# A hybrid transformer layer: the transfers that sum weight blocks are placed behind attention weight splits, and the second feed-forward product splits two pieces ahead

## The chip, the cores and the metric

The kernel runs on one core of a Trainium2 chip. TensorE (PE) multiplies, VectorE (DVE), ScalarE (ACT) and GpSimd (POOL) work on vectors, SyncE (SP) issues most transfers; POOL and ACT can issue transfers too. The metric is the device time of one launch in microseconds (us), as a median over runs.

## The reference, cut to what matters

One layer over 512 latent tokens with a context prefix of 256 tokens, width 1024, all in float32.

```python
h_lat = modulate(x, norm1_g, sh1, sc1)            # adaLN, from c
h_ctx = modulate(ctx, norm1_g, csh1, csc1)        # from c_ctx
p_lat, p_ctx = h_lat @ w_in, h_ctx @ w_in         # z, xBC, dt, q, k, v, gates
ssd = ssd_output(ssd_bidir(...), xs, z, d_skip, g)   # bidirectional state-space mixer
att = window_ctx_attention(q, k, v, kc, vc, sink)    # window 128, all context keys
x = x + gt1 * (g_ssd * (ssd @ w_o_ssd) + g_att * (att @ w_o_att)) @ w_out
u = dwconv(modulate(x, norm2_g, sh2, sc2) @ w_up)    # 1024 -> 2 x 2816, 3 taps along tokens
x = x + gt2 * ((silu(u[:, :2816]) * u[:, 2816:]) @ w_down)
return rmsnorm(x, final_g)
```

## The kernel before

**Products.** Activations lie transposed, channels on partitions and tokens along the free axis. A float32 product is made of three float32r products: weight and activation are each split into a high part and a low part (high x high, high x low, low x high). For a weight tile this is `split`: ACT casts the raw tile to the high part (`whi`, L172), DVE subtracts it from the raw tile (`wlo`, L173). A raw tile is 128 x 1024, 512 KB, loaded by SP (`load_raw`, L166) into one of three buffers; `whi` and `wlo` have two buffers each.

**Start.** A plan written in Python (class `Plan`, with costs and due times per step) fixes the order of PE, ACT and DVE up to the first products: 16 loads of modulation weights (`wm`, L460), 8 of the input (`xsb`), 8 of a first block of gate columns (`w`), two of the context, then the first q and k weights (`wraw<-wq`, `wraw<-wk`) and the tables. Modulation rows come out of PE (L506), are copied (`tm`, L510) and turned into columns (L514); the inputs are scaled by them (`ah`, `al`), and the gate product runs on them (L556) before the RMS factor is known. POOL raises the two means to the power -0.5 (L594). ACT takes the tanh of five gate tiles (L618) in two alternating buffers `tb`, each of which SP writes to DRAM (`ts_d`, L619). Then come the normed context (`hch`, L548), the first k and q, and v.

**Attention.** A second plan orders 16 blocks of attention (scores L935, row minimum L944, exponential L951, norm of the rows L966, transposes L971, values L984) beside 30 projection products: q 2 to 7, k 1, z and the attention output. Each of these splits its weight in `high` (ACT, L1065) and `low` (DVE, L1068), and `high` issues the next weight's load. q and k rows are copied within the on-chip memory by SP (L832, L867); the plan counts 6 us for them. After it come the state-space part, with POOL's first work there at L1483 and broadcasts `fb` of decay rows from DRAM (L1552), then the output products, the up product (L216 to L219 with `mh`, `ml`) and the down product.

**Down product.** It is not done as one matrix product. The two halves of the tokens and of the 2816 and 1024 channels make blocks, and seven block products with sums of operands take the place of eight. The sums of activations are made on DVE (`f_sums`, `f_split`). The sums of weight blocks are made by transfers from DRAM to DRAM: `weight_sums` issues 32 of them on POOL's queue, 704 KB each, 16 of which copy a block into `DSUMS` and 16 of which add another block to it there (`accum_op`). It is called where the plan of the start has been written out; a scheduler orders POOL's queue, and there nothing holds the transfers back but each other:

```python
for q in range(4):
    G.dma_start(DSUMS[j][q], first[q])                              # L152
for q in range(4):
    G.dma_start(DSUMS[j][q], more[q], accum_op=ALU.add, ...)        # L154
```

`down_step(j, q)` runs block product j for one of four output tiles: two weight pieces of 6 and 5 tiles (`DPARTS`), 33 matmuls of 256 columns (`product`, L1960 to L1962). `down_last` takes the eight pieces of the last block product at once and ends with the final norm and the output. `run` walks the program of steps: before a step is written out, its pieces and one more have been loaded and split.

Of the kernel before, what the change touches and what calls it, by code (L numbers as in the profile page):

```python
# [10 lines left out]
F32R = mybir.dt.float32r  # L11
U8 = mybir.dt.uint8
AF = mybir.ActivationFunctionType
ALU = mybir.AluOpType
# [4 lines left out]
P = 128  # L19
# [4 lines left out]
EPS = 1e-6  # L24
# [6 lines left out]
V_FG = 64  # L31
# [8 lines left out]
def raw(ap):  # L40
    return ap.bitcast(F32)
# [3 lines left out]
def tile_hybrid_layer(  # L45
# [31 lines left out]
    V, S, G, T = nc.vector, nc.scalar, nc.gpsimd, nc.tensor  # L77

    cpool = ctx.enter_context(tc.tile_pool(name="cpool", bufs=1))
    wpool = ctx.enter_context(tc.tile_pool(name="wpool", bufs=2))  # L80
    hpool = ctx.enter_context(tc.tile_pool(name="hpool", bufs=1))
# [24 lines left out]
    def accb():  # L106
        return bank("acc")

    def misb():
        return bank("mis")  # L110
# [3 lines left out]
    def tmp(tag):  # L114
        return tpool.tile([P, 512], F32, tag=tag, name=tag, bufs=TMP[tag])
# [23 lines left out]
    DK = NFF // 2  # L139
    DPARTS = ((0, 6), (6, DK - 6))  # L140
    DSUMS = {i: dpool.tile([4, P, DK * P], F32, name="dsum%d" % i) for i in (1, 2, 4, 5)}
# [2 lines left out]
            for u, (k0, n) in enumerate(DPARTS):  # L144
                src["dn", (4 * j + q) * 2 + u] = t[:, k0 * P : (k0 + n) * P], n * P

    def weight_sums():
        for j, first, more in (
            (4, wdn[0], wdn[2]), (1, wdn[2], wdn[3]), (2, DSUMS[4], wdn[3]), (5, DSUMS[2], wdn[1]),
        ):  # L150
            for q in range(4):
                G.dma_start(DSUMS[j][q], first[q])  # L152
            for q in range(4):
                G.dma_start(DSUMS[j][q], more[q], accum_op=ALU.add, max_dma_last_dim=DK * P)  # L154

    M_LOADS = {}

# [12 lines left out]

    def split(r, n, hi, lo):
        S.copy(hi[:, :n], r[:, :n])  # L172
        V.tensor_tensor(lo[:, :n], r[:, :n], raw(hi[:, :n]), ALU.subtract)  # L173

    ELSEWHERE = {}

    def load(key):
        r, n = load_raw(key)
        if key[0] == "m":
            return r  # L180
        if key in ELSEWHERE:
            hi, lo = ELSEWHERE[key]()
            split(r, n, hi, lo)
            return hi, lo
        hi = wpool.tile([P, 1024], F32R, tag="whi", name="whi", bufs=2)
        lo = wpool.tile([P, 1024], F32R, tag="wlo", name="wlo", bufs=2)
        split(r, n, hi, lo)
        return hi, lo

    def run(prog, early=None):  # L190

        seq = [k for keys, _ in prog for k in keys]
        have, nload, nuse = {}, 0, 0
        for keys, fn in prog:
            nuse += len(keys)
            while nload < min(nuse + 1 + (early in keys), len(seq)):
                have[seq[nload]] = load(seq[nload])
                nload += 1
            fn(*[have.pop(k) for k in keys])
# [49 lines left out]
    def col(base, i):  # L249
        return vec[:, base + i : base + i + 1]  # L250
# [6 lines left out]
    def rms_sums(ps, part, nblk, c, first, last, late=False):  # L257
        for i in range(nblk):
            m = T.matmul(
                ps[:, i : i + 1], part[:, i * P : (i + 1) * P], rmsc[:, c : c + 1],  # L260
                start=first and i == 0, stop=last, skip_group_check=True,
            )
            if i == 0 and late:
                tc.keep_in_program_order(m)

    def rms_root(ps, nblk, eps):
        rs = cpool.tile([P, 4], F32, tag="rs", name="rs", bufs=2)
        ms = cpool.tile([P, 4], F32, tag="ms", name="ms", bufs=2)
        V.tensor_scalar_add(ms[:, :nblk], ps[:, :nblk], eps)  # L269
        G.tensor_tensor(rs[:, :nblk], ms[:, :nblk], phalf[:, :nblk], ALU.pow)  # L270
        return rs
# [110 lines left out]
    hll = hpool.tile([P, KT, L], F32R, tag="hll", name="hll")  # L382
# [17 lines left out]
    first = {}  # L400
    gates = []
    with tc.tile_pool(name="spool", bufs=1) as sp:
# [38 lines left out]
        first_, B_ = Plan(), {}  # L441
# [14 lines left out]
        mod_raw, w0_raw, wh, wl, hi_, lo_, rows, raws, ws = {}, {}, {}, {}, {}, {}, {}, {}, {}  # L456
# [101 lines left out]
        def product(j, i, t):  # L558
            h = (hi_.get(j), lo_.get(j)) if j < NU else (hlh[:, j, :], hll[:, j, :])

            n = 3 * NU if j < NU else 3 * KT
            part(pg[i], ("P", i), n, [w[j][:, i * P : (i + 1) * P] if j in w else None for w in (wh, wl)], h, t)
# [21 lines left out]
        def sums(x, q, n):  # L584
            B_["p" + x] = accb()
            rms_sums(B_["p" + x], q, n, 0, True, True)
# [51 lines left out]
        r = {}  # L638
        cq = tmp("te")[:, :LC]
        for j in range(KT):  # L640
# [46 lines left out]
            x = ("hi", "lo") if j >= NU else ("hh", "hl")  # L687
# [31 lines left out]
        for n in range(2):  # L719
            for j in range(KT):  # L720
                x = ("hi", "lo") if j >= NU else ("hh", "hl")
# [6 lines left out]
        run_plan(first_.order({"PE": 5.2, "ACT": 3.0, "DVE": 3.6, "SP": 0.7}, bus=2.76))  # L728
        first.update(w=ws[1], q=B_[0, "g"], k=B_[1, "g"])
    dump("h", raw(hlh[:, 0, :]))  # L730
    weight_sums()

# [119 lines left out]
    Q, F = {}, {}  # L854
# [187 lines left out]
    def product_atoms(g, key, accs):  # L1042

        kind, t = key
        d, R, G_ = {}, 1e6 + 100 * g, "%d" % g
# [19 lines left out]
            S.copy(d["w"][0], d["r"])  # L1065

        def low():
            V.tensor_tensor(d["w"][1], d["r"], raw(d["w"][0]), ALU.subtract)  # L1068

        def rope_part(f):  # L1070
            scale = -0.125 if kind == "k" else 1.0
# [35 lines left out]
        last, late = "G%s.7" % G_, g >= OLD  # L1107
# [524 lines left out]
    for g in range(4):  # L1632
        s = ssd_steps(g)
# [106 lines left out]
    HL = L // 2  # L1740
    HALF = [slice(0, HL), slice(HL, L)]
# [196 lines left out]
    def x_add(c, u, a, ps):  # L1938
        x = x1[c // 4][:, c % 4, HALF[u]]
        g = ng2[:, c - 4 : c - 3] if a < 0 else mod2[:, 24 + c : 25 + c]  # L1940
        V.scalar_tensor_tensor(x, ps, g, x, ALU.mult, ALU.add)

    def half_square(c, u):
        x, q = x1[c // 4][:, c % 4, HALF[u]], q3[:, HALF[u]]
        if c % 4 == 0 and (c, u) in ((0, 0), (4, 1)):
            S.activation(q, x, AF.Square)
        else:
            sq = tmp("tc")[:, :HL]
            S.activation(sq, x, AF.Square)
            V.tensor_tensor(q, q, sq, ALU.add)  # L1950
# [49 lines left out]

        return [("dn", (4 * j + q) * 2 + u) for u in range(2)], fn

    def down_last(*ws):

        ws = [ws[2 * q : 2 * q + 2] for q in range(4)]
        scaled, r = {}, {}

        def finish(u):

            z = HALF[u]  # L2010
            tail = u == 0
            r3 = rms_spread(r["s"], 2)
            if tail:
                r3s = tmp("tc")[:, :HL]
                S.copy(r3s, rms_spread(r["s"], 2)[:, :HL])
            for i, cs in enumerate(((0,), (1,), (4,), (2, 3), (5,), (6,), (7,)) if tail else ((0, 1), (2, 3), (4, 5), (6, 7))):
                for c in cs:
                    x = x1[c // 4][:, c % 4, z]
                    if tail and c in scaled:
                        G.tensor_tensor(x, scaled[c], r3s, ALU.mult)  # L2020
                    else:
                        V.scalar_tensor_tensor(x, x, col(V_FG, c), r3[:, :HL], ALU.mult, ALU.mult)
                n, c = len(cs), cs[0]
                tc.keep_in_program_order((S if c in ((1, 2, 6) if tail else (2,)) else nc.sync).dma_start(
                    out[c * P : (c + n) * P, z].rearrange("(a p) t -> p a t", a=n), x1[c // 4][:, c % 4 : c % 4 + n, z]
                ))
                yield

        pf = misb()

        def sums(u, part, first, last):
            rms_sums(pf[:, 2 * u : 2 * u + 2], part, 2, 0, first, last)

        def root():
            sums(1, q3[:, HALF[1]], True, True)
            r["s"] = rms_root(pf[:, 2:4], 2, EPS)

        def spread():
            r["f"] = finish(1)
            next(r["f"])  # L2040
            next(r["f"])

        def early():
            sums(0, q3[:, HALF[0]], False, False)
            for _ in r["f"]:
                pass

        with tc.manual_schedule(engines={mybir.EngineType.PE}):
            for q in range(4):
                ps = accb()  # L2050
                product(6, q, ws[q], ps[:, :HL], True, {1: {2: root}, 2: {2: spread}, 3: {6: early}}.get(q, {}))
                if q < 3:
                    x_add(4 + q, 0, -1, ps[:, :HL])
                    half_square(4 + q, 0)
                    if q < 2:
                        scaled[4 + q] = tmp("te")[:, :HL]
                        S.activation(scaled[4 + q], x1[1][:, q, HALF[0]], AF.Copy, scale=col(V_FG, 4 + q))
            xo, sq = x1[1][:, 3, HALF[0]], tmp("tc")[:, :HL]
            for b in range(2):
                z = slice(b * P, (b + 1) * P)  # L2060
                V.scalar_tensor_tensor(xo[:, z], ps[:, z], ng2[:, 3:4], xo[:, z], ALU.mult, ALU.add)
                S.activation(sq[:, z], xo[:, z], AF.Square)
            sums(0, sq, False, True)
            r["s"] = rms_root(pf[:, 0:2], 2, EPS)
            for _ in finish(0):
                pass

    run(
        [([], lambda: (y_split(range(8)), [square(True) for _ in range(4)], y_split(range(8, 12))))]
# [6 lines left out]
        + [([("out", o) for o in (5, 6, 7)], out_last), ([], close_c1)]  # L2076
        + weave([up_step(t) for t in range(NFF)], msteps[24:])
        + [down_step(j, q) for j in range(6) for q in range(4)]
        + [([("dn", 48 + i) for i in range(8)], down_last)],
        early=("g", 15),  # L2080
    )

# [83 lines left out]
```

## Time and profile before

| | |
|---|---|
| median of three runs | 1310.0 us (1309.07 to 1311.47) |
| profiled execution | 1307.86 us, its span 1306.1 us |
| busy: PE | 1248.7 us, 96% |
| busy: DVE, ACT, POOL | 924.3, 686.8, 169.1 us |
| POOL's transfers (q0) | 23.07 MB, 7.4% of the 16 DMA engines' span |
| SP's transfers (q1) | 181.32 MB, 44.6% |

The profile is of one execution. Busy times of PE come from modelled ends of pipelined matmuls, so a full PE is not PE at its peak. "Granted clock" is the TensorE clock as a share of full speed. A line of a view of waits reads: who waited, for whom, us in total, times, longest. The idle time of an engine that is not the bound costs nothing.

### The profile page before, as it was taken

The numbers are of one execution on the slowest core, as the hardware profiler recorded it, in microseconds if no ns is written. First come the engines' busy times: TensorE is split into PE (matmuls) and PEld (weight loads), VectorE is DVE, ScalarE is ACT, GpSimd is POOL, SyncE is SP. The second block draws the span as 40 slices with busy tenths as digits, with TensorE's granted clock in tenths as the row PEclk, the third lists the DMA queues.
The fourth block names the chain that finished last, engine by engine and source line by source line (L and its number), as shares of the span: only waits on it lengthen the run. The fifth ranks groups of instructions, "written<-read, shape, count | busy, mean of one in ns | idle before, by whom it ended". The sixth has DMA issues, their size and how long they took to land.

```text
span 1306.1 us, 18420 instructions
## 1 busy us (share of the span) xinstructions
PE 1248.7 (96%) x6790; PEld 1037.5 (79%) x6790; DVE 924.3 (71%) x1518; ACT 686.8 (53%) x1289; POOL 169.1 (13%) x177
## 2 busy tenths in 40 slices
PE   6667999999999999999999999999999999999997
PEld 4445888888888887877877778888988888889997
DVE  1244478878877358969789676777677777777785
ACT  1224477878774445648657475222543434344563
POOL 2121000000000003425244262000200000000000
PEclk7788899999999999999999999999999999999999
DMA  9999831432224723644635657777323333336553
GB/s 292 310 322 299 198 89 55 129 105 78 73 79 133 205 98 97 168 140 113 194 104 165 200 161 247 251 234 233 115 97 113 113 113 113 113 115 203 176 169 105
DMA packets 104761, 206.35 MB, mean 158 GB/s; under 512 B 8928, under 2 KB 52768, under 8 KB 104416
## 3 DMA queue, kind: packets, MB, share of 16 engines
q1 hardware_dynamic: 94736, 181.32, 44.6%
q0 software_dynamic: 8960, 23.07, 7.4%
q8 instruction: 53, 0.87, 0.3%
q10 hardware_dynamic: 976, 0.79, 0.2%
q14 instruction: 36, 0.29, 0.1%
HBM read 182.54 MB, written 40.17 MB: 171 GB/s over the span
## 4 chain that ended last, share of the span: by engine, by line
PE 89%; DMA 9%; ACT 1%; DVE 1%; issue 0%; SPq 0%; POOL 0%; DVEq 0%; ACTq 0%; POOLq 0%
PE acc L216 19%; PE acc L219 19%; PE acc L217 19%; PE score L935 3%; PE po L984 3%; DMA xsb<-xT 2%; PE pt L971 2%; PE mis L1588 2%; DMA wraw<-wq 2%; DMA wm<-wm 2%; PE mis L1481 2%; PE acc L1962 2%; PE acc L1960 2%; PE acc L1961 2%; DMA ts_d<-tb 1%; PE mis L1596 1%
## 5 line engine op out<-in xcount | busy, mean ns | idle before, releaser
L172 ACT CAST whi<-wraw 128x1024 fp32r<-128x1024 f32 (+2 forms) x133 | 132.5, 997 | 174.6 <-PE acc L217 121.3
L173 DVE TENSOR_TENSOR wlo<-wraw,whi 128x1024 fp32r<-128x1024 f32 (+2 forms) x133 | 157.1, 1182 | 81.0 <-ACT whi L172 78.5
L216 PE MATMUL acc<-hlh,whi 128*128 128x512 f32 x472 | 195.4, 414 | 2.1 <-ACT whi L172 2.1
L217 PE MATMUL acc<-hll,whi 128*128 128x512 f32 x472 | 186.0, 394 | 0.0
L219 PE MATMUL acc<-hlh,wlo 128*128 128x512 f32 x472 | 185.8, 394 | 0.0
L216 PE MATMUL acc<-mh,whi 128*128 128x512 f32 x368 | 143.3, 390 | 0.0
L217 PE MATMUL acc<-ml,whi 128*128 128x512 f32 x368 | 143.2, 389 | 0.0
L219 PE MATMUL acc<-mh,wlo 128*128 128x512 f32 x368 | 143.2, 389 | 0.0
L216 PEld LDWEIGHTS acc<-hlh,whi 128*128 128x128 f32 x472 | 89.4, 189 | 20.5 <-issue 3.1
L219 PEld LDWEIGHTS acc<-hlh,wlo 128*128 128x128 f32 x472 | 89.1, 189 | 20.0 <-DVE wlo L173 0.3
L217 PEld LDWEIGHTS acc<-hll,whi 128*128 128x128 f32 x472 | 89.5, 190 | 17.6 <-issue 2.4
L1483 POOL TENSOR_TENSOR st<-st,eT 128x512 f32<-128x512 f32 x24 | 28.9, 1206 | 435.0 <-ACT st L1500 420.7
L217 PEld LDWEIGHTS acc<-ml,whi 128*128 128x128 f32 x368 | 69.1, 188 | 14.4
L219 PEld LDWEIGHTS acc<-mh,wlo 128*128 128x128 f32 x368 | 69.1, 188 | 14.3
L216 PEld LDWEIGHTS acc<-mh,whi 128*128 128x128 f32 x368 | 69.1, 188 | 14.3
L270 POOL TENSOR_TENSOR rs<-ms,phalf 128x2 f32<-128x2 f32 (+1 forms) x5 | 4.8, 954 | 469.1 <-DVE ms L269 469.1
L216 PE MATMUL acc<-hch,whi 128*128 128x256 f32 x176 | 55.6, 316 | 8.4 <-ACT hch L548 8.4
L944 DVE CUSTOM_DVE_ANT_0 p<-score,winm,nsink 128x512 f32<-128x512 f32 (+1 forms) x64 | 51.9, 811 | 15.4 <-PE score L935 13.9
L1369 DVE SCALAR_TENSOR_TENSOR ta<-acc,half,ta 128x511 f32<-128x511 f32 (+1 forms) x66 | 43.9, 665 | 25.8 <-ACT ta L1368 25.6
L1368 ACT ACTIVATE ta<-acc,half 128x512 f32<-128x512 f32 (+1 forms) x66 | 46.9, 711 | 22.6 <-PE acc L219 21.1
L951 ACT ACTIVATE p<-p,mneg 128x512 f32<-128x512 f32 (+1 forms) x64 | 49.7, 777 | 15.4 <-DVE mneg L944 14.8
L979 DVE TENSOR_TENSOR ptl<-pt,pth 128x512 fp32r<-128x512 f32 x72 | 47.5, 686 | 8.6 <-ACT pth L975 7.7
(399 smaller groups left out, 3188.3 us busy)
## 6 DMA issues: line engine op xcount, KB each, us to landing
wraw<-wup SPq DMA_DIRECT2D x44, 512.0 KB, 3.6
dsum<-wdn POOLq DMA_DIRECT2D x24, 704.0 KB, 19.1
fb<-cs_d SPq DMA_DIRECT2D x32, 512.0 KB, 6.3
wraw<-wm SPq DMA_DIRECT2D x32, 512.0 KB, 4.0
wraw<-wx SPq DMA_DIRECT2D x24, 512.0 KB, 3.6
wm<-wm SPq DMA_DIRECT2D x16, 512.0 KB, 17.5
wraw<-wz SPq DMA_DIRECT2D x16, 512.0 KB, 3.7
wraw<-wos SPq DMA_DIRECT2D x16, 512.0 KB, 4.7
```

What stands on the lines that cost most here:

```text
L172: S.copy(hi[:, :n], r[:, :n])
L173: V.tensor_tensor(lo[:, :n], r[:, :n], raw(hi[:, :n]), ALU.subtract)
L216: T.matmul(ps, wh, xh[:, k0 + k, :], start=a, stop=False)
L217: T.matmul(ps, wh, xl[:, k0 + k, :], start=False, stop=False)
L219: T.matmul(ps, wl, xh[:, k0 + k, :], start=False, stop=b)
L935: T.matmul(ps[:, o : o + len(z) * P], Q[h][:, b * P : (b + 1) * P], k[:, j, z[0] * P : (z[-1] + 1) * P], start=v == 0 and o % 512 in (0, P ...
L944: V.tensor_tensor_reduce(p[:, :w], d["ps"][i][:, o0 : o0 + w], m, op0=ALU.add, op1=ALU.min, scale=1.0, scalar=nsink[:, h : h + 1], accum_o ...
L951: S.activation(p, p, AF.Exp, bias=d["mneg"][:, i : i + 1], scale=-1.0, accum_out=d["den"][:, i : i + 1])
L979: V.tensor_tensor(d["ptl"][x], d["pt"][x], raw(d["pth"][x]), ALU.subtract)
L984: T.matmul(d["po"], vst[:, cols[x], j, :], d[y][x], start=x == 0 and y == "pth", stop=x == c - 1 and y == "ptl")
L1368: S.activation(o[:, :n], ps[:, :n], AF.Identity, scale=hcol(base_w, stride + i), bias=hcol(base_b, i))
L1369: V.scalar_tensor_tensor(o[:, 1:n], ps[:, 0 : n - 1], hcol(base_w, i), o[:, 1:n], ALU.mult, ALU.add)
```

## The change

It has two parts.

The first removes `weight_sums`. The same 32 transfers, in the same order, stand in a list, and `sum_step` issues the next of them with a dependency on a given DVE instruction. It is called with the low half of each of the 30 attention weights (`low`) and of state-space weights (key `"x"` in `load`) until the list is empty.

The second concerns the down product. `run` loads and splits two pieces ahead of a down step instead of one. Every other pair of pieces gets split tiles of its own (`dnw`, two pieces of high and low part), in the memory that the low part of the up product's activations held (tag `hll`). `down_last` becomes four steps with two pieces each in place of one with eight; its final part stays under a fixed order of PE.

```diff
-    def weight_sums():
-        for j, first, more in (
...
+    SUMS = []
+    for j, first_, more in (
+        (4, wdn[0], wdn[2]), (1, wdn[2], wdn[3]), (2, DSUMS[4], wdn[3]), (5, DSUMS[2], wdn[1]),
+    ):
+        SUMS += [(DSUMS[j][q], first_[q], {}) for q in range(4)]
+        SUMS += [(DSUMS[j][q], more[q], dict(accum_op=ALU.add, max_dma_last_dim=DK * P)) for q in range(4)]
+    BEHIND = mybir.DependencyInfo(mybir.DependencyClass.Sync, mybir.DependencyReason.DATA)
+
+    def sum_step(ins):
+        if SUMS:
+            o, x, how = SUMS.pop(0)
+            dma = G.dma_start(o, x, **how)
+            tc.add_manual_dep(dma.ins, ins.ins.name, BEHIND, reason="weight sums behind a split")
...
     def split(r, n, hi, lo):
         S.copy(hi[:, :n], r[:, :n])
-        V.tensor_tensor(lo[:, :n], r[:, :n], raw(hi[:, :n]), ALU.subtract)
+        return V.tensor_tensor(lo[:, :n], r[:, :n], raw(hi[:, :n]), ALU.subtract)
...
-        hi = wpool.tile([P, 1024], F32R, tag="whi", name="whi", bufs=2)
-        lo = wpool.tile([P, 1024], F32R, tag="wlo", name="wlo", bufs=2)
-        split(r, n, hi, lo)
+        if key[0] == "dn" and key[1] % 4 > 1:
+            if "dnw" not in F:
+                F["dnw"] = hpool.tile([P, 2, 2, 6 * P], F32R, tag="hll", name="dnw")
+            hi, lo = (F["dnw"][:, key[1] % 2, i, :] for i in range(2))
+        else:
+            hi = wpool.tile([P, 1024], F32R, tag="whi", name="whi", bufs=2)
+            lo = wpool.tile([P, 1024], F32R, tag="wlo", name="wlo", bufs=2)
+        low = split(r, n, hi, lo)
+        if key[0] == "x":
+            sum_step(low)
...
-            while nload < min(nuse + 1 + (early in keys), len(seq)):
+            ahead = 1 + (early in keys) + any(k[0] == "dn" for k in keys)
+            while nload < min(nuse + ahead, len(seq)):
...
-    weight_sums()
...
         def low():
-            V.tensor_tensor(d["w"][1], d["r"], raw(d["w"][0]), ALU.subtract)
+            sum_step(V.tensor_tensor(d["w"][1], d["r"], raw(d["w"][0]), ALU.subtract))
...
-    def down_last(*ws):
+    def down_last():
...
+        return [([("dn", 48 + 2 * q + i) for i in range(2)], lambda *w, q=q: last(q, w)) for q in range(4)]
...
-        + [([("dn", 48 + i) for i in range(8)], down_last)],
+        + down_last(),
```

More of the change, by code (lines that the diff above doesn't have):

```diff
@@ L145, in tile_hybrid_layer @@
                 src["dn", (4 * j + q) * 2 + u] = t[:, k0 * P : (k0 + n) * P], n * P
-    def weight_sums():
-        for j, first, more in (
[L149 to L154, printed above, removed]
+    SUMS = []
[10 more added lines that the diff above has]
+            tc.add_manual_dep(dma.ins, ins.ins.name, BEHIND, reason="weight sums behind a split")
     M_LOADS = {}
@@ L2001, in down_step @@
         return [("dn", (4 * j + q) * 2 + u) for u in range(2)], fn
-    def down_last(*ws):
-        ws = [ws[2 * q : 2 * q + 2] for q in range(4)]
+    def down_last():
         scaled, r = {}, {}
@@ L2027, in finish @@
                 yield
-        pf = misb()
         def sums(u, part, first, last):
-            rms_sums(pf[:, 2 * u : 2 * u + 2], part, 2, 0, first, last)
+            rms_sums(r["pf"][:, 2 * u : 2 * u + 2], part, 2, 0, first, last)
         def root():
             sums(1, q3[:, HALF[1]], True, True)
-            r["s"] = rms_root(pf[:, 2:4], 2, EPS)
+            r["s"] = rms_root(r["pf"][:, 2:4], 2, EPS)
         def spread():
@@ L2046, in early, with last @@
                 pass
[L2048 to L2066, printed above, removed]
+        def last(q, w):
+            if q == 0:
+                r["pf"] = misb()
+            ps = accb()
+            product(6, q, w, ps[:, :HL], True, {1: {2: root}, 2: {2: spread}, 3: {6: early}}.get(q, {}))
+            if q < 3:
+                x_add(4 + q, 0, -1, ps[:, :HL])
+                half_square(4 + q, 0)
+                if q < 2:
+                    scaled[4 + q] = tmp("te")[:, :HL]
+                    S.activation(scaled[4 + q], x1[1][:, q, HALF[0]], AF.Copy, scale=col(V_FG, 4 + q))
+                return
+            with tc.manual_schedule(engines={mybir.EngineType.PE}):
+                xo, sq = x1[1][:, 3, HALF[0]], tmp("tc")[:, :HL]
+                for b in range(2):
+                    z = slice(b * P, (b + 1) * P)
+                    V.scalar_tensor_tensor(xo[:, z], ps[:, z], ng2[:, 3:4], xo[:, z], ALU.mult, ALU.add)
+                    S.activation(sq[:, z], xo[:, z], AF.Square)
+                sums(0, sq, False, True)
+                r["s"] = rms_root(r["pf"][:, 0:2], 2, EPS)
+                for _ in finish(0):
+                    pass
+        return [([("dn", 48 + 2 * q + i) for i in range(2)], lambda *w, q=q: last(q, w)) for q in range(4)]
     run(
```

## The prediction

> **What bounds the kernel now.** I read the page first, then busy time by stage, then the waits of the start, then the DMA issues there.
>
> ```profile
> span 1306.1 us, 18420 instructions
> ...
> DMA  9999831432224723644635657777323333336553
> ...
> q0 software_dynamic: 8960, 23.07, 7.4%
> ```
>
> The DMA row is full in the first four of the 40 slices (32.7 us each) and never again. q0 is POOL's queue, and the 32 weight sums are all it carries: 7.4% of 1306.1 us is 96.7 us of all 16 DMA engines, 3.0 us a sum.
>
> ```profile
> 0.00:97.80 97.80, 62.94 (x332) 41.49 (x332) 27.90 (x64) 21.07 (x44) 21.17 (x35) 0.76 1.05 308
> 97.80:120.40 22.60, 21.41 (x82) 17.28 (x83) 12.88 (x24) 10.93 (x19) 1.52 (x3) 0.83 1.17 295
> 120.40:138.00 17.60, 7.08 (x28) 5.13 (x26) 8.75 (x19) 10.31 (x19) 4.59 (x5) 0.65 1.05 267
> 138.00:166.90 28.90, 28.73 (x168) 27.05 (x169) 11.72 (x18) 9.63 (x21) 0.00 (x0) 0.92 0.74 188
> 166.90:440.00 273.10, 273.02 (x1458) 231.15 (x1458) 212.87 (x431) 201.06 (x386) 0.00 (x0) 1.00 0.32 97
> ...
> 1179.00:1300.00 121.00, 116.39 (x947) 114.37 (x945) 91.20 (x145) 66.28 (x101) 1.40 (x2) 1.00 0.54 165
> ```
>
> Columns: stretch, its length, busy time of PE, weight loads, DVE, ACT, POOL, then granted clock, DMA share, GB/s. Four stretches make the start: to the landing of the first attention weight (97.8), to the end of the first products, to the first split of a second weight, to the first score (166.9). There PE works at a reduced clock and idles 34.9 us in the first stretch and 10.5 in the third, with DMA over 1.0. From 166.9 to 440 (attention) PE is full at clock 1.00 and DMA at 0.32. So DMA bounds the start, PE the rest; the last row is the second feed-forward product.
>
> ```profile
> 2.58 14.63 DMA xsb<-xT
> ...
> 73.21 24.56 DMA wraw<-wq
> ```
>
> The chain that ended last says the same: from 2.58 to 97.8 us it is five loads, one behind the other, of which these are the first and the last.
>
> ```profile
> dsum<-wdn POOLq DMA_DIRECT2D x20, 704.0 KB, 21.2
> wm<-wm SPq DMA_DIRECT2D x16, 512.0 KB, 17.5
> ...
> wraw<-wup SPq DMA_DIRECT2D x29, 512.0 KB, 3.5
> ```
>
> DMA issues, with the us to landing last: first two lines 0 to 97.8 us, the third 1000 to 1160 us, where no sum runs. The same 512 KB lands in 17.5 us beside the sums and in 3.5 without them.
>
> **The change, part by part.**
>
> *The sums move.* In the built program all 32 transfers on POOL's queue now wait for a DVE subtraction: 30 behind the attention weights' low halves (L1068), two behind the first two weights of the state-space part (L173). None is left before attention, and the two small powers on POOL (L594) come ahead of them.
>
> First stretch. SP loads 14.8 MB up to the first attention weight (16 x 512, 8 x 320, 8 x 256, 2 x 512, 512 and 92 KB). The rate for SP alone is that of the row below, 17.83 MB in 35.6% of 160 us, 313 GB/s.
>
> ```profile
> q1 hardware_dynamic: 4896, 17.83, 35.6%
> ```
>
> 14.8 MB then take 47 us, and with the first issue and one landing of 3.5 us the weight is there at about 51 instead of 97.8. PE needs 62.94 x 0.76 = 48 us at full clock for what it did in this stretch, so PE and DMA are near each other, and neither hides the other wholly: the loop from modulation rows to columns to scaled operand has waits of its own. I take 55 us: 43 us less. Bounds: 51, if PE keeps up, and 70, if PE stays at 0.76 (62.9 plus some 7 until the first operand is there).
>
> ```profile
> ACT tb L618 <- DMA ts_d<-tb: 13.8, 3, 7.1
> ...
> PE acc L216 <- ACT hch L548: 8.4, 1, 8.4
> ```
>
> The other three stretches, 69.1 us. ACT's gates (L618) write two alternating buffers to DRAM and waited 13.8 us for those writes; behind them stood the context operand (hch), for which PE waited 8.4 us. Writes of that size land in 2.0 us where no sum runs (next fence), so this goes. The work is 21.41 x 0.83 + 7.08 x 0.65 + 28.73 x 0.92 = 49 us at full clock. I take 51 of the 69.1: 18 us less; bounds 12 and 20. What is late next is PE itself and, in the third stretch, ACT's 10.31 us.
>
> *Attention gets the sums.* 96.7 us of DMA over 273 us are 0.35, with 0.32 already there 0.67 in the mean. Who could wait: ACT's split for its load, and the scores for copied q and k rows.
>
> ```profile
> wraw<-wz SPq DMA_DIRECT2D x13, 512.0 KB, 3.7
> ...
> zs_d<-te SPq DMA_DIRECT2D x15, 256.0 KB, 2.0
> ```
>
> ```profile
> L1065 ACT CAST whi<-wraw x30: 1026/1041/1061, 161.7 to 427.7; 128x1024 fp32r<-128x1024 f32 x30
> ...
>   PE acc L884: 7.2, 1
> ```
>
> (The first two are issues between 180 and 440 us; then come all 30 splits of attention weights with what ended ACT's idle time before them.) Not one of 30 splits waited for a load: there are three raw buffers, and PE's use of the split tiles sets the pace. A sum costs nothing there as long as a load slips by a few us. POOL has nothing else queued: the last two sums go behind the two DVE splits below, and POOL's first work after them is at 498 us, so a sum that waits for DVE delays only later sums.
>
> ```profile
> 433.73 1.23 DVE L173 TENSOR_TENSOR wlo<-wraw,whi 128x1024 fp32r<-128x1024 f32 x1 [3.70 <-ACT whi L172]
> ...
> 439.28 1.23 DVE L173 TENSOR_TENSOR wlo<-wraw,whi 128x1024 fp32r<-128x1024 f32 x1 [4.33 <-ACT whi L172]
> ```
>
> ```profile
> 498.30 1.06 POOL L1483 TENSOR_TENSOR st<-st,eT 128x512 f32<-128x512 f32 x1 [367.75 <-ACT st L1500]
> ...
> DMA to landing us min/median/max: 4.9/6.3/10.0
> ```
>
> The tight place is the end. The two splits are 5.6 us apart, the last sums are accumulating ones, and right behind them ACT needs the first broadcasts of the decay rows (fb, L1552, whose landings are the last row). If the median landing of 6.3 doubles for two of them, that is 13 us on ACT and less on PE, which has products between. I take 3 us; bounds 0 and 13.
>
> A rule speaks against the place. Row first: in attention DVE runs tensor_scalar on p (L966).
>
> ```profile
> L966 DVE TENSOR_SCALAR p<-p,es 128x640 f32<-128x640 f32 x16 | 8.2, 550 | 0.1
> L154 POOL DMA_DIRECT2D dsum<-wdn x16: 1005/1020/1103, 8.8 to 129.5; - x16
> ```
>
> The Trainium skill, page "SBUF — State Buffer", section "Who interferes with whom", says that DVE in a two-port mode and GpSimd lock each other out, and that descriptors of a POOL transfer are written through that port. No run here shows it. It becomes a rival below.
>
> *Two pieces ahead in the second feed-forward product.* Odd pairs of pieces get tiles of their own, so a split can be done a piece sooner.
>
> ```profile
> PE acc L1960 <- ACT whi L172: 2.0, 3, 0.9
> ```
>
> PE's largest wait for splits in 1179 to 1300 us is 2.0 us in all, and 4.6 us of PE are idle there (121.00 less 116.39), part of it the final norm. ACT (66 of 121 us) and DVE (91) do the same work. The new tile takes the place of the first product's low operand, so its first split waits for the last matmul of that product (1179 us), and is needed one product later. I take 3 us less; bounds 0 and 4.6. Opening the last step into four adds no instruction on PE, and the final norm stays.
>
> *Sum.* 43 + 18 + 3 - 3 = 61 us. The profiled execution took 1307.86 us (span 1306.1); the median of three runs is 1310.0, 2.1 above. 1307.9 - 61 = 1246.9, with 2.1: 1249 us.
>
> **Rivals.** A measurement can tell 0.2%, 2.6 us, from no change.
>
> *The start stays cold.* Nothing but DMA improves, PE keeps 0.76 and the first stretch takes 70 us: 15 us less gain, the second group 14 instead of 18: 1249 + 19 = 1268. For it: the first operand passes PE, ACT and DVE in small steps, and PE waits in each. Against it: with loads at twice the pace those waits have more matmuls beside them.
>
> *The start runs warm.* Loads at the best pace and PE at full clock.
>
> ```profile
> 10.00:20.00 10.00, 4.19 (x17) 3.96 (x18) 1.96 (x9) 1.60 (x3) 4.99 (x7) 0.50 0.95 258
> ```
>
> Where PE waits the clock is 0.50, as in this row of the start; where it is dense, as in the row of attention above, 1.00. If denser loads keep it dense, the first stretch takes 47 (47 us of loads with nothing added) and the others 49, 10 us more gain, with the other terms at 0 and 4.6, 1249 - 15 = 1234. The Trainium skill, "TensorE: Matmul & The Clock Gate", Part 1, says that a window of about 3.4 us decides: busy gives full rate, idle half. The two rows agree with it.
>
> *Sums crowd attention.* The fb loads and late splits cost the bound of 13 instead of 3: 1259.
>
> *POOL's descriptors hold DVE.* Each of 32 sums could stop DVE for the 1.02 us of its descriptors (row L154): 33 us if each hits and DVE is always late, 1282. Against it: those 16 instructions of L966 are busy 8.2 us, so few would meet.
>
> *Slower.* In attention the six q tiles from the third on and the second k are copied by SP before their scores. If those copies were held up as the weights of the start were, 17.5 instead of 3.7 us, 13.8 later, and the plan's 6 us for them hid 2.3 of it, PE would lose 11.5 us seven times, 80 us: 1329. It turns slower once each loses over 9 us. It needs DMA near 1.0 throughout; 0.67 speaks against.
>
> *The change does nothing*, if sums still ran early: the queue order excludes it nearly.
>
> **How the numbers follow.** Forecast (1240 to 1258) 0.56; cold start 0.19; warm start 0.12; crowded attention 0.06; descriptors 0.03; slower 0.03; nothing 0.01. The range goes from 1234, the warm case, to 1271, the cold case with some crowding, and leaves out the last three cases, half of the warm one and the tail where cold and crowded add up: some 0.17. Faster by over 0.2%: 0.56 + 0.19 + 0.12 + 0.06 + 0.03 = 0.96, same 0.01, slower 0.03.
>
> **What would show it.** In the changed kernel the DMA row should fall below 9 within the first two slices, the first attention weight land near 51 us, the first score start near 106, ACT's wait for ts_d nearly vanish, q0 spread from about 105 to 390 us, and the splits L1065 still wait for PE, not for loads. The product waits of the last stretch should be under 1 us. I am wrong if the first stretch takes over 70 us, if PE's idle time in attention grows by over 13 us, or if DVE's groups there get longer.

## The result, and the profile after

The changed kernel takes 1239.8 us (median of four runs, 1237.6 to 1240.6) beside 1309.5 us before (four runs, 1308.4 to 1311.5): a ratio of 0.9463, 95% interval 0.9446 to 0.9481, 69.7 us less. The forecast was 1249, its range 1234 to 1271. The profiled execution took 1237.59 us, 2.2 below the median. First the page of the changed kernel, the rows that answer to those of before.

```profile
span 1235.8 us, 18429 instructions
...
PE   9999999999998999999999999999999999999997
...
PEclk9999999999999999999999999999999999999998
DMA  9645585745798346346356568676133433337662
...
q0 software_dynamic: 8960, 23.07, 8.3%
```

DMA is full in the first slice (30.9 us each), falls to 6 in the second and reaches 9 again only from 340 to 371 us, where the last sums run. PE is below 9 in the slice behind that one and in the last. The sums move the same 23.07 MB. The chain of work that ended last and the loads of modulation weights say the same in one line each, also from the page:

```profile
PE 96%; DMA 2%; DVE 1%; ACT 1%; issue 0%; SPq 0%; POOL 0%; DVEq 0%; ACTq 0%; POOLq 0%
...
wm<-wm SPq DMA_DIRECT2D x16, 512.0 KB, 8.3
```

The chain no longer begins with five loads but with matmuls, and a load of modulation weights lands in 8.3 us (median) where it took 17.5.

PE runs nearly as many matmuls in each part as before (6790 in all, in both) and in nearly one order, so windows can be laid from one matmul to the same matmul in the other kernel. Busy time by stage of the kernel before, cut so:

```profile
0.00:166.73 166.73, 119.99 (x606) 90.79 (x607) 61.10 (x123) 51.94 (x99) 27.28 (x43) 0.79 1.01 281
166.73:438.40 271.67, 271.59 (x1453) 230.02 (x1452) 212.30 (x431) 199.73 (x385) 0.00 (x0) 1.00 0.32 96
438.40:458.30 19.90, 19.90 (x103) 16.95 (x103) 9.21 (x12) 10.86 (x23) 0.00 (x0) 1.00 0.76 217
458.30:865.40 407.10, 407.10 (x2167) 320.37 (x2166) 312.88 (x458) 231.28 (x501) 130.80 (x120) 1.00 0.53 165
865.40:1178.80 313.40, 313.40 (x1521) 264.83 (x1520) 235.25 (x345) 126.37 (x181) 8.19 (x10) 1.00 0.41 131
1178.80:1300.30 121.50, 116.67 (x948) 114.51 (x946) 91.50 (x146) 66.41 (x102) 1.40 (x2) 1.00 0.53 164
```

And of the changed kernel, the start in two pieces (landing of the first attention weight, first score):

```profile
0.00:42.30 42.30, 41.17 (x300) 29.36 (x301) 23.61 (x56) 21.21 (x43) 1.79 (x10) 1.00 0.98 371
42.30:94.64 52.34, 52.34 (x309) 46.85 (x309) 36.89 (x68) 31.04 (x56) 1.45 (x2) 1.00 0.50 155
94.64:366.30 271.66, 271.58 (x1453) 230.02 (x1452) 212.28 (x431) 199.53 (x385) 22.28 (x30) 1.00 0.64 172
366.30:393.00 26.70, 22.63 (x103) 18.41 (x103) 8.50 (x11) 9.86 (x21) 1.79 (x2) 0.87 1.03 242
393.00:800.00 407.00, 407.00 (x2167) 320.33 (x2166) 312.51 (x459) 231.58 (x502) 132.32 (x120) 1.00 0.54 166
800.00:1113.40 313.40, 313.40 (x1521) 264.88 (x1520) 235.39 (x345) 126.06 (x181) 8.20 (x10) 1.00 0.41 130
1113.40:1230.00 116.60, 114.50 (x948) 113.68 (x947) 90.48 (x146) 66.26 (x102) 1.40 (x2) 0.99 0.56 171
```

Column by column (length, then PE's count in brackets): the start shrinks from 166.73 to 94.64, 72.1 us less. Attention stays at 271.7 though its DMA share (the last column but one) doubles from 0.32 to 0.64. The next 103 matmuls take 26.7 instead of 19.9: 6.8 us lost. The two long stages do not move. The second feed-forward product goes from 121.5 to 116.6, 4.9 us less. That is 72.1 - 6.8 + 4.9 = 70.2 of the 70.3 us by which the spans differ.

The lost 6.8 us have a view of their own, the waits of the changed kernel between 366.3 and 393 us (us in all, times, longest):

```profile
ACT E L1584 <- DMA fb<-cs_d: 13.6, 2, 10.3
DVE ta L1382 <- ACT ta L1381: 12.7, 1, 12.7
...
PE mis L1409 <- DVE BT L1390: 4.0, 1, 4.0
```

ACT waits 13.6 us for the broadcasts of the decay rows (fb), DVE behind ACT, PE behind DVE for 4.0. One-microsecond windows of the same place show where the remaining 2.7 go:

```profile
382.00:383.00 1.00, 0.00 (x0) 0.00 (x0) 0.60 (x1) 0.31 (x1) 0.00 (x0) 0.66 1.13 229
388.00:389.00 1.00, 1.00 (x4) 0.79 (x3) 0.00 (x0) 0.96 (x4) 0.00 (x0) 0.50 0.65 186
389.00:390.00 1.00, 1.00 (x6) 0.83 (x5) 0.42 (x1) 1.00 (x3) 0.00 (x0) 0.93 1.23 325
```

PE stands from 380.1 to 384.1 us. Its clock falls to 0.50 at about 382.3, is still 0.50 in the second row, and is back at about 389.1. So the first five microseconds of work after the wait run at half clock: matmuls of 512 columns start 0.43 us apart there, and 0.23 us apart from 389.2 on. The wait is paid a second time. The Trainium skill, "TensorE: Matmul & The Clock Gate", Part 1, has it so: an idle window of about 3.4 us puts the clock to half, and a busy one of that length brings it back. The rows agree in part: the half clock lasted 6.8 us, two such windows, but it began 2.2 us after PE's last matmul ended (a modelled end), before a whole 3.4 us of idling.

### The profile page after: what moved, and what is told of

Its sections match the earlier page's. It is cut to its first block, busy times and chain, and to the rows that moved or that the text cites. A ratio compares the mean times of both kernels' runs of the same rounds, so it can differ in the third digit from the quotient of the medians.

```text
span 1235.8 us, 18429 instructions
## 1 busy us (share of the span) xinstructions
PE 1222.6 (99%) x6790; PEld 1023.5 (83%) x6790; DVE 921.5 (75%) x1518; ACT 685.8 (55%) x1289; POOL 170.6 (14%) x177
## 3 DMA queue, kind: packets, MB, share of 16 engines
q0 software_dynamic: 8960, 23.07, 8.3%
## 4 chain that ended last, share of the span: by engine, by line
PE 96%; DMA 2%; DVE 1%; ACT 1%; issue 0%; SPq 0%; POOL 0%; DVEq 0%; ACTq 0%; POOLq 0%
PE acc L230 19%; PE acc L233 19%; PE acc L231 19%; PE score L948 3%; PE po L997 3%; PE pt L984 2%; PE mis L570 2%; PE mis L1601 2%; PE mis L1494 2%; PE acc L1973 2%; PE acc L1975 2%; PE acc L1974 2%; PE mis L1609 1%; PE mis L1974 1%; PE mis L1973 1%; PE mis L1975 1%
## 5 line engine op out<-in xcount | busy, mean ns | idle before, releaser
L178 ACT CAST whi<-wraw 128x1024 fp32r<-128x1024 f32 (+3 forms) x118 | 120.0, 1018 | 151.0 <-PE acc L231 111.8
L179 DVE TENSOR_TENSOR wlo<-wraw,whi 128x1024 fp32r<-128x1024 f32 (+3 forms) x118 | 142.9, 1211 | 66.5 <-ACT whi L178 64.1
L231 PEld LDWEIGHTS acc<-hll,whi 128*128 128x128 f32 x472 | 89.4, 189 | 17.5 <-issue 2.4
L964 ACT ACTIVATE p<-p,mneg 128x512 f32<-128x512 f32 (+1 forms) x64 | 49.7, 777 | 15.4 <-DVE mneg L957 14.8
L159 POOL DMA_DIRECT2D dsum<-wdn x24 | 20.7, 861 | 241.0 <-DVE wlo L1081 222.4
```

The source lines that it names most:

```text
L179: return V.tensor_tensor(lo[:, :n], r[:, :n], raw(hi[:, :n]), ALU.subtract)
L231: T.matmul(ps, wh, xl[:, k0 + k, :], start=False, stop=False)
L964: S.activation(p, p, AF.Exp, bias=d["mneg"][:, i : i + 1], scale=-1.0, accum_out=d["den"][:, i : i + 1])
```

## The experiments

Eight kernels, in two groups of four, each group beside runs of the kernel before on its own chip (medians 1308.8 and 1308.7). "Start", "attention" and so on are the stages of the windows above, cut at the same matmuls.

**One part alone: the sums.** The feed-forward part of the change is put back, the sums stay behind the splits.

```diff
-            ahead = 1 + (early in keys) + any(k[0] == "dn" for k in keys)
+            while nload < min(nuse + 1 + (early in keys), len(seq)):
...
-        + down_last(),
+        + [([("dn", 48 + i) for i in range(8)], down_last)],
```

> Only the first part of the change: the 32 weight sums wait behind the weight splits, the second feed-forward product stays as before. Theory (the parts add: start 72.1 us less, 6.7 us lost in front of the state-space part, 5.3 us less in the second feed-forward product by the matched matmuls of the two traces): 65.4 us less than before, 1244 beside a before of 1309.5, about 5 us over the changed kernel. Rival (the 5.3 us come from where the sums' loads now find the DMA engines, not from the second part): as fast as the changed kernel, 1239.

Measured 1247.1 us, ratio 0.9519 (0.9503 to 0.9535): slower than the changed kernel by a difference of ratios of 0.0056, 7 us; the spans of the profiled executions (1241.5 and 1235.8) differ by 5.7. The first score comes at 94.4 us, and the last product takes as long as before:

```profile
1113.90:1235.00 121.10, 116.51 (x947) 114.55 (x946) 91.15 (x145) 66.28 (x101) 1.40 (x2) 1.00 0.54 165
```

By the profiled spans this part gives 64.6 us and the other, below, 3.8, together 68.4 of 70.3: the parts add to within 2 us. The theory's 1244 lies 3 below the median; the five runs spread from 1243.2 to 1248.0, and the profiled one took 1243.3. The rival, as fast as the changed kernel, falls.

**The other part alone: two pieces ahead.** The sums go back to where they were.

```diff
+    weight_sums()          # all 32 at once, after the plan of the start
...
-        low = split(r, n, hi, lo)
-        if key[0] == "x":
-            sum_step(low)
+        split(r, n, hi, lo)
```

> Only the second part: the splits of the second feed-forward product run two pieces ahead, the sums start at once as before. Theory: 5.3 us less than before, 1304, and the waits of the product for its splits gone from the stretch after the last matmul of the first product. Rival (the prediction's bound of 4.6 us was right and the rest belongs to the sums): 0 to 4.6 us less, 1305 to 1309.5.

Measured 1303.0 us, ratio 0.9950 (0.9938 to 0.9963): faster by 5 to 8 us. Its profiled start is 1.0 us longer than before, its last product is the changed kernel's to 0.1 us:

```profile
1179.80:1296.40 116.60, 114.54 (x948) 113.72 (x947) 90.58 (x146) 66.40 (x102) 1.40 (x2) 0.99 0.56 171
```

So this part is worth 4.9 us, over the bound of 4.6. Of the 4.9, PE's idle time gives 2.7 (121.50 - 116.67 = 4.8 before, and 2.1 for the changed kernel, 116.60 - 114.50) and its busy time 2.2. The starts of the matmuls show how busy time can shrink. Two that follow each other in the product before:

```profile
1185.71 0.28 PE L1961 MATMUL mis<-fs,whi 128*128 128x256 f32 x1
1186.06 0.39 PE L1962 MATMUL mis<-fs,wlo 128*128 128x256 f32 x1
```

The usual distance between two starts is 0.12 us, and here it is 0.35; but the first matmul counts as busy for 0.28 of them, so only 0.07 shows as idle. In the product before, 43 matmuls start late in this way, by 5.9 us in all; in this run 4 do, by 0.3. A part of the old waits stood inside matmuls that counted as busy.

**Two sums behind each of the first ten splits.**

```diff
-        if SUMS:
+        for _ in range(min(len(SUMS), 2 if len(SUMS) > 12 else 1)):
```

> The changed kernel, but two sums instead of one wait behind each of the first ten attention splits, so that all 32 are issued by the 22nd split and none behind a split of the state-space part. Theory (the 6.7 us that PE loses between attention and the state-space part come from the last accumulating sums beside the first broadcasts of the decay rows, and attention has room for more sums): that loss goes to under 1 us, attention stays at 271.7 us, 1233. Rival (the loss is due to the broadcasts themselves, now that the start is shorter): it stays, 1239.8. Second rival (two at a time crowd the loads of attention): attention grows by more than the 6.7 us saved, 1240 to 1250.

Measured 1230.5 us, ratio 0.9397 (0.9384 to 0.9410): faster than both kernels, its interval below that of the changed kernel. Attention and the 103 matmuls behind it:

```profile
94.23:365.90 271.67, 271.58 (x1453) 229.88 (x1452) 212.46 (x431) 199.64 (x385) 23.48 (x30) 1.00 0.67 180
365.90:385.80 19.90, 19.90 (x104) 16.95 (x103) 9.12 (x12) 10.76 (x23) 0.00 (x0) 1.00 0.81 238
```

The loss is gone to the last tenth (19.90 as before the change), ACT's wait for fb is 2.8 us, and attention did not grow. The last sums beside the fb broadcasts were the cause. The spans differ by 7.5 us, of which these 103 matmuls are 6.8; the medians differ by 9.3, and what makes the rest no stretch shows.

**All 32 at the first attention split.**

```diff
-        if SUMS:
+        for _ in range(len(SUMS)):
```

> The changed kernel, but all 32 sums wait behind the first attention split and run one behind the other from there. It asks if it is the place of the sums (beside a stage that PE bounds) or their pace (one per split) that makes them cheap. Theory of the place: weight loads have 10 to 35 us of slack in attention, so loads that land in some 17 us instead of 4 cost nothing, PE loses at most a few us, and the 6.7 us at the end go: 1233 to 1240. Theory of the pace: DMA is full from about 92 to 235 us, copies of q and k and some weights come late as in the stretches of the start before, 16.8 us or more are lost: 1250 to 1310.

Measured 1231.7 us, ratio 0.9407 (0.9394 to 0.9420), as fast as two at a time.

```profile
94.15:150.00 55.85, 55.85 (x330) 48.76 (x329) 44.96 (x97) 45.39 (x92) 12.17 (x16) 1.00 1.11 285
150.00:200.00 50.00, 50.00 (x269) 42.66 (x268) 41.80 (x83) 42.00 (x79) 10.41 (x12) 1.00 1.08 293
200.00:366.80 166.80, 165.81 (x858) 138.37 (x857) 125.67 (x253) 112.33 (x214) 0.00 (x0) 1.00 0.38 111
```

DMA is over full (share above 1) for 105 us, a sum takes 16.9 us to land in the median, and PE has no idle time in the first two rows and 1.0 us in the third. It is the place that made the sums cheap, not their pace: attention has weights, copies and stores under way far enough ahead that nothing on PE's path is late.

**The kernel before without sums.** The loads of the second feed-forward product take unsummed weights of the same size.

```diff
-    weight_sums()
...
-        for j, t in enumerate((wdn[0, q], DSUMS[1][q], DSUMS[2][q], wdn[1, q], DSUMS[4][q], ...
+        for j, t in enumerate((wdn[0, q], wdn[2, q], wdn[3, q], wdn[1, q], wdn[2, q], ...
```

> The kernel before without the 32 weight sums (the second feed-forward product then reads unsummed weights, of the same size, so that its result differs). Theory (the sums cost their price in the start and nothing else there was cured by the change; in attention they cost nothing): the first score comes at 94.3 us as in the kernels with moved sums, 72 us are gained, 1236 to 1237, and the kernel with two sums behind each of the first ten splits is faster by just the 5 us of the second part, though it does carry all the sums. Rival (sums in attention cost some us that no stretch showed): this one is as fast as that kernel or faster, 1231 or below.

Measured 1237.4 us, ratio 0.9451 (0.9436 to 0.9466), 71 to 72 us less; first score at 94.5.

```profile
0.00:94.50 94.50, 92.81 (x606) 75.32 (x607) 60.65 (x123) 52.25 (x99) 2.49 (x11) 1.00 0.72 252
```

Taking the sums away from the old kernel gives the same start as moving them, and the kernel that carries all of them, two at a time, is 6.9 us faster by the medians (5.5 by the spans), where the second part gives 4.9. In attention the sums cost nothing that these runs can show.

**Eight sums left in the start.**

```diff
     dump("h", raw(hlh[:, 0, :]))
+    for o, x, how in SUMS[:8]:
+        G.dma_start(o, x, **how)
+    del SUMS[:8]
```

(The other 24 go behind the attention splits, two at a time behind the first five of them.)

> The changed kernel with the first 8 sums (4 plain, 4 accumulating) issued at once, as before, and the others two behind each of the first splits of attention. By the price of one plain (1.7 us of all 16 engines) and one accumulating (4.3 us) sum these are 24 of the 96.7 us. Theory (the start before was bound by DMA, a sum costs its DMA time there): 18 (the same share of 72) to 24 us over 1230.5, 1248 to 1255. Rival (PE sets the start now, and DMA has room behind the first weight): under 9 us, below 1240. Second rival (a sum in flight delays every load behind it by more than its own time): over 30 us, above 1260.

Measured 1254.7 us, ratio 0.9583 (0.9567 to 0.9598), 24.2 us over the kernel with all of them moved. The first attention weight lands at 64.7 us, 22 later than in the changed kernel, and the first score starts at 118.9, 24.6 later than with all sums moved. The queues up to 66 us:

```profile
q1 hardware_dynamic: 5952, 15.90, 65.8%
q0 software_dynamic: 2240, 5.77, 37.0%
```

37.0% of 66 us are 24.4 us of all 16 engines, beside the 24.6. In this run the sums in the first stretch cost their DMA time, one to one; PE hides none of it.

**All 32 at the first split of the start**, 54 us in, behind the loads of the first stretch.

```diff
             def weight(n, part):
...
-                V.tensor_tensor(ws[n][1], raws[n][0], raw(ws[n][0]), ALU.subtract)
+                low = V.tensor_tensor(ws[n][1], raws[n][0], raw(ws[n][0]), ALU.subtract)
+                if n == 0:
+                    sum_step(low)      # lets all 32 go
```

> The changed kernel with all 32 sums behind the first weight split of the start (low half done at about 54 us), 40 us ahead of the first score, one behind the other. Theory (the second to fourth stretch of the start have a chain through DRAM, gates written and read back, that pays for full DMA queues, the 16.8 us that the change gained there): 10 to 17 us over the kernel that lets them all go at the first attention split, 1242 to 1249. Rival (only the loads of the first stretch pay): the same 1232.

Measured 1259.4 us, ratio 0.9621 (0.9604 to 0.9637): 27.7 us over the burst at the first attention split, more than either expected. The first score comes at 110.3, 16 later than with the burst at the first attention split, which the theory had (10 to 17); the rest is lost in the first 25 us of attention. Waits from 54 to 136 us:

```profile
DVE hcl L564 <- ACT hch L562: 12.6, 2, 9.7
ACT tb L632 <- DMA ts_d<-tb: 12.2, 3, 6.9
ACT whi L1080 <- DMA wraw<-wq: 10.0, 1, 10.0
```

The first two are the chain of the gates through DRAM that the start had before. The third is new: a q weight was asked for at 111.7 us and its cast waited 10 us for it. The copies of k and q made PE wait too (4.4, 2.1 and 1.5 us there). Begun 40 us earlier, the same burst meets transfers that have no time in hand.

**Half the modulation weights.** Every second load is left out, its tile used twice.

```diff
+            if i % 2:
+                mod_raw[i] = twice[i - 1]
+                return
-            t = mod_raw[i] = sp.tile([P, 4, 256], F32, tag="wm", name="wm", bufs=6)
+            t = mod_raw[i] = twice[i] = sp.tile([P, 4, 256], F32, tag="wm", name="wm", bufs=6)
```

> The changed kernel without every second load of modulation weights (the tile of the first is used twice, so that the result differs): 4.2 of some 15 MB are not loaded in the first 42 us. Theory (with the sums gone PE is dense from 1 us on, 41.2 of 42.3 us at clock 1.00, and sets the start): the first score comes at most 1.5 us earlier. Rival (DMA, 98% busy there, still sets it): it comes up to 11 us earlier, 4.2 MB by 0.38 MB per us.

The first score comes at 93.75, 0.9 us earlier (a single run, 1236.3 us).

```profile
0.00:42.30 42.30, 41.04 (x304) 29.56 (x305) 24.26 (x59) 21.61 (x44) 1.79 (x10) 1.00 0.84 305
```

DMA falls from 0.98 to 0.84 in this row and PE's count rises from 300 to 304: with the sums gone PE sets the start, and fewer bytes buy nothing.

## Why the prediction was right, and where its sizes were off

*The mechanism* held: the start was bound by DMA, the sums held it up, and attention carries them free. Sign and range were right. The forecast was 9 us too high, and the case's own range of 1240 to 1258 missed the median by 0.2.

*First stretch.* 55 us was taken, with 51 as the lower bound; the weight landed at 42.3. The term was mis-sized by 12 to 13 us and the bound itself was wrong. It was built on 313 GB/s, worked out from the stretch 1000 to 1160 us, where SP's queue is busy a third of the time. In the start of the changed kernel, 0 to 42.3 us, the same queue does better:

```profile
q1 hardware_dynamic: 5804, 15.66, 97.3%
```

15.66 MB in 97.3% of 42.3 us are 380 GB/s, so the 14.8 MB need 39 us, not 47. Why a packet costs more time in the later stretch these runs do not tell. The kernel's own plan had a figure near the measured one: `load_atom` prices a load at 381 KB per us, which is 390 GB/s. The kernel before held a better price for the term in its own stretch, the queues from 0 to 97.8 us:

```profile
q0 software_dynamic: 4861, 14.78, 58.9%
```

58.9% of 97.8 is 57.6 us of sums, and 55.5 is what left. That a sum there costs its DMA time was then shown with eight of them. The addition for PE (clock 0.76, small steps that wait) was wrong in the other direction too: once loads come in time PE is busy 41.2 of 42.3 us at clock 1.00. Over the whole start PE is busy 93.5 of 94.6 us; its own work sets that time now, as the run with half the modulation weights bears out. The rival of the warm start, 0.12, is what the start did, in its clock; its first stretch (47) was still too long.

*The other three stretches.* 51 taken, 52.3 measured (42.30 to 94.64). ACT's wait for ts_d fell from 13.8 to 0.3 us and PE's 8.4 us for hch went, as said.

*Attention.* The stretch itself cost 0 where 3 was taken for it and the place behind it; the tight place was named rightly, and its price was 6.8. The 13 us on ACT were right (13.6). What was too small was the share that reaches PE: 4.0 us of idling, and then 2.7 us at a low clock, which the sum did not count for a wait of that length.

The splits of attention still wait for PE and for no load, as the line of their casts shows (with what ended ACT's idle time before them):

```profile
L1078 ACT CAST whi<-wraw x30: 1027/1041/1063, 89.6 to 355.6; 128x1024 fp32r<-128x1024 f32 x30
...
  PE acc L897: 7.2, 1
```

*Two pieces ahead.* 3 taken, bounds 0 and 4.6, 4.9 measured. The upper bound counted only PE's idle time; 2.2 us came out of busy time, where late starts had hidden.

In sum the errors are 72.1 - 61 = 11.1 more from the start, 3.8 more lost behind attention and 1.9 more from the last part: 9.2 us, as 70.2 is to 61. That the total came this close is luck in part, since the loss behind attention stands against the gain in the start.

*The rivals.* Of the sums that crowd attention (1259) only the fb part came, at half its price. The rule of the Trainium skill, "SBUF — State Buffer", section "Who interferes with whom", by which POOL's descriptors and DVE lock each other out, left no mark on the group that it would hit first. Groups of attention before (busy us, mean ns):

```profile
L966 DVE TENSOR_SCALAR p<-p,es 128x512 f32<-128x512 f32 (+1 forms) x32 | 15.3, 516 | 0.2
```

and in the changed kernel, with 30 sums beside them:

```profile
L979 DVE TENSOR_SCALAR p<-p,es 128x512 f32<-128x512 f32 (+1 forms) x32 | 15.4, 518 | 0.2
```

The instructions on POOL that issue the sums did not get longer beside DVE's work either: 1103 ns at most before (L154), 1097 after.

```profile
L159 POOL DMA_DIRECT2D dsum<-wdn x24: 486/1008/1097, 92.2 to 369.0; - x24
```

So neither side shows a lock in these rows; how often a sum and an instruction of that group met was not counted. The rival on the slower side (1329) needed DMA near 1.0 throughout attention. The burst gave that for 105 us and lost 1 us, so its price was wrong in that place. The burst in the start shows that its mechanism exists where copies and weights are asked for late.

## What to carry to other kernels

In this kernel bulk transfers that are needed late belonged beside a stage that a compute engine bounds and whose own loads run well ahead; the same 32 transfers cost 72 us in the start, 6.8 us where their tail met loads that are asked for just in time, and nothing measurable in between. Price a transfer that leaves a DMA-bound stretch by its own queue's share in that stretch, not by a rate from elsewhere, and then ask what the next engine's full-speed time is. End a spread of transfers well ahead of the next just-in-time load: two at a time gave 1230.5 us in place of 1239.8.

## What was not expected of the hardware

PE's clock recovers fully once its work comes in time: 0.79 before and 1.00 after over the start, with nearly the same matmuls (606 and 607). DMA that is over full (share 1.08 to 1.11 for 105 us) cost a PE-bound stage 1 us, while a single wait of 4.0 us on PE cost 6.8, because 5 us of work behind it ran at half clock. And busy time of matmuls can hold waits: 2.2 us of it went when the splits came sooner, beside the 2.7 us that were shown as idle.
